# Key lengths in RWKV-7 on Trainium2: a product with block-diagonal ones in place of a product, a broadcast and a transpose

## The chip, the cores and the metric

One core of one Trainium2 chip runs the whole program. The core has five engines that run side by side, each through its own list in order: TensorE (PE, with its weight loads shown apart as PEld), VectorE (DVE), ScalarE (ACT), GpSimd (POOL) and SyncE (SP, which here only issues transfers). The metric is the time of one execution on the device in microseconds (us); lower is better.

## The reference, cut to what matters

Two layers of a decoder with three groups of heads; the change touches the RWKV-7 group alone (6 heads of 64 channels, 2048 tokens). Its part of the reference:

```python
kk = heads(k * k_k)
kk = kk / jnp.maximum(jnp.sqrt(jnp.sum(kk * kk, axis=-1, keepdims=True)), 1e-12)
k = k * (1.0 + (a - 1.0) * k_a)
r, k, v, a = heads(r), heads(k), heads(v), heads(a)
decay = jnp.exp(-jnp.exp(heads(w)))
y = _wkv7_scan(r, decay, k, v, -kk, kk * a)
```

`kk` is the removal key: each head's key, divided by its length. The scan uses it twice, as `-kk` and as `kk * a`; the kernel leaves one of the two undivided and puts the whole factor, one over the squared length, on the other.

## The kernel before, in words

Each layer has a first phase, `phase_a`, and then attention and the output projection. `phase_a` projects the input (each projection is 24 or 16 matmuls on line L441, into one of two PSUM banks), and beside that runs the RWKV group. Everything is written as chains, Python generators that yield the time at which they may go on, and `weave` picks the chain that is due next by a modelled clock (`clk`), in which each piece of work has a written cost. The order in which the chains are picked is the order of the instructions on PE, which is kept as written; the order on DVE, ACT and POOL is set by the scheduler of the tile framework. So a changed cost or a wait that is gone moves PE's whole order from that place on.

The RWKV group has these chains: `rwkv_prep` (a preparation: 128 tokens, so 4 for each block of 512 tokens, 16 for each layer, 32 in all), `rwkv_chunks` (two chunks of 64 tokens for each preparation), `rwkv_inv` (a triangular inverse, many small DVE rows, L689 and L691), `rwkv_run` (the state, one chunk after another) and `rwkv_out`. A block's fourth preparation comes late in the block's projections (`PACE`), near the next block's `norm`, in which PE transposes the normed input (L370) and DVE splits it (L269).

A preparation keeps channels on partitions and tokens along the row: a tile `[128, 3, 128]`, two heads on the 128 partitions, three such pairs. The sum over a head's 64 channels is therefore a sum over partitions, which PE makes. Before, `sq` (the squared key) is the stationary side and `ones2` (128 x 2) the moving side (L546), so that tokens come out on partitions, 6 numbers each. DVE bounds and inverts these (L548, L549), ACT spreads each over 64 columns (L551, `nb`), and PE transposes `nb` back (L592) into a PSUM bank `nps`. DVE multiplies that with `ke` into half of `bd` (L610); the other half is L611. Two more PE steps end a preparation: the product for the bonus (L620, of `rk`, which DVE makes on L617) and the transpose of `v` (L628). `bd` goes to the chunks' first product (L647). All small PSUM tiles of this chain take one of two banks (`MB`).

Of the kernel before, what the change touches and what calls it, by code (L numbers as in the profile page):

```python
# [10 lines left out]
F32 = mybir.dt.float32  # L11
# [3 lines left out]
AF = mybir.ActivationFunctionType  # L15
ALU = mybir.AluOpType
# [20 lines left out]
NP = RH // 2  # L37
# [14 lines left out]
RSB, XB, TRB = 6, 3, 7  # L52
# [7 lines left out]
MB, LMB, CHB, YB, PJ, HT = (0, 1), (2,), (3,), (4,), (5, 6), (7,)  # L60
# [130 lines left out]
def trunk(tc, a, out):  # L191
# [7 lines left out]
    def mk(p, shape, tag, dt=F32, bufs=None):  # L199
        return p.tile(list(shape), dt, name=tag, tag=tag, bufs=bufs)  # L200

    cst = pool(top, "cst")
# [6 lines left out]
    ident = cst.tile([128, 128], F32, name="ident")  # L209
    P.memset(ident, 0.0)  # L210
    P.affine_select(ident, ident, [[1, 128]], ALU.not_equal, 1.0, base=0, channel_multiplier=-1)
    ones2 = cst.tile([128, 2], F32, name="ones2")
    V.memset(ones2, 0.0)
    V.memset(ones2[0:64, 0:1], 1.0)
    V.memset(ones2[64:128, 1:2], 1.0)
    ones1 = cst.tile([128, 1], F32, name="ones1")
    V.memset(ones1, 1.0)
    mhalf = cst.tile([128, 1], F32, name="mhalf")
# [75 lines left out]
    def phase_a(l, rq_t, near, far, flags):  # L294
# [26 lines left out]
        for h in range(2):  # L321
            sl = HEADS[h]
# [186 lines left out]
        def rwkv_prep(j, u, q2, xin):  # L509
# [31 lines left out]
            t_ta = banks.give(b1, clk.a(128, e, times=3))  # L541
            yield from banks.wait(MB, 1, lambda: t_sq)

            sps, b = banks.get(MB, [128, 6])
            for p_ in range(NP):
                T.matmul(sps[:, 2 * p_:2 * p_ + 2], sq[:, p_], ones2, start=True, stop=True)  # L546
            n2 = mk(rt, [128, 6], "n2")
            V.tensor_scalar(n2, sps, 1e-24, None, ALU.max)  # L548
            V.reciprocal(n2, n2)  # L549
            nb = mk(rt, [128, 6, 64], "tr", bufs=TRB)  # L550
            A.activation(nb, n2.unsqueeze(2).to_broadcast([128, 6, 64]), AF.Copy, scale=-0.5)  # L551
            t = banks.give(b, clk.v(6, clk.pe(650)))
            t_nb = clk.a(384, clk.v(40, t))
            t = clk.v(384, clk.v(192, t_th))
            t_em = clk.a(460, t, times=2)
            V.tensor_scalar(th, th, 1.0, None, ALU.add)
# [29 lines left out]
                V.tensor_scalar(km[:, p_], ta[:, p_], ka[:, p_:p_ + 1], ka1[:, p_:p_ + 1], ALU.mult, ALU.add)  # L586
            V.tensor_tensor(km, km, k, ALU.mult)
            t_km = clk.v(384, clk.v(180, t_ta, times=3))
            yield from banks.wait(MB, 1, lambda: t_nb)
            nps, b = banks.get(MB, W3)  # L590
            for p_ in range(NP):
                T.transpose(nps[:, p_], nb[:, 2 * p_:2 * p_ + 2].rearrange("p a b -> p (a b)"), ident)  # L592
            e = clk.pe(330)
            t_ke = clk.v(384, max(t_ta, t_em), times=2)
            t_bd = banks.give(b, clk.v(384, max(t_ke, t_km, e), times=6))
            ke = mk(rt, W3, "tr", bufs=TRB)
            V.scalar_tensor_tensor(ke, ta, 1.0, kq, ALU.add, ALU.mult)
            V.tensor_tensor(ke, ke, em, ALU.mult)
# [2 lines left out]
            def c4(x):  # L601
                return x.rearrange("p a (c t) -> p c a t", c=2)
# [4 lines left out]

            bd = mk(rt, [128, 2, NP, 2, CH], "bd", bufs=2)
            for h, sl in enumerate(HEADS):
                V.tensor_tensor(bd[sl, :, :, h], c4(nps)[sl], c4(ke)[sl], ALU.mult)  # L610
                V.tensor_tensor(bd[sl, :, :, 1 - h], c4(km)[sl], c4(em)[sl], ALU.mult)  # L611
            yield lambda: done["out"] >= len(halves) - 2
            t_rk = clk.v(384, t_km)
# [121 lines left out]
        def rwkv_run(cur, s0, s1, y, odd):  # L735

            W = [128, NP, CH]
            xs1 = mk(rt, W, "x1")
            yield from banks.wait(CHB, 1, lambda: cur["t"])
            ps, b = banks.get(CHB, [128, 2, NP, CH])  # L740
            for p_ in range(NP):
                by_head(ps[:, 0, p_], cur["ar"][:, p_, 0], s0[:, p_], start=True, stop=True)
            V.tensor_tensor(xs1, ps[:, 0], cur["xv"], ALU.add)
            yield clk.v(192, clk.pe(520))
            for p_ in range(NP):
                by_head(ps[:, 1, p_], cur["T"][:, p_], xs1[:, p_], start=True, stop=True)
            uv = cur["uv"]
            for h, sl in enumerate(HEADS):
                V.tensor_copy(uv[sl, :, h], ps[sl, 1])
            t = banks.give(b, clk.v(192, clk.pe(520), times=2))  # L750
            yield from banks.wait(CHB, 1, lambda: t)
            ps, b = banks.get(CHB, [128, 2, NP, CH])
            for p_ in range(NP):
                for h, sl in enumerate(HEADS):
                    T.matmul(ps[sl, 0, p_], cur["bk"][:, p_, sl], uv[:, p_, h], start=True, stop=True)
            sp_ = mk(rt, W, "sp")
            V.tensor_tensor(sp_, ps[:, 0], s0, ALU.add)
            V.tensor_tensor(s1, sp_, cur["pc"].unsqueeze(2).to_broadcast(W), ALU.mult)
            t = clk.v(192, banks.give(b, clk.v(192, clk.pe(520))))
            yield from banks.wait(YB)  # L760
            py, b = banks.get(YB, [128, NP, CH])
            outs_ = [HEADS[(h + odd) % 2] for h in range(2)]
            for p_ in range(NP):
                for sl, so in zip(HEADS, outs_):
                    T.matmul(py[so, p_], cur["ar"][sl, p_, 1], s0[sl, p_], start=True, stop=False)
                for h, so in enumerate(outs_):
                    T.matmul(py[so, p_], cur["mr"][:, p_, h], uv[:, p_, h], start=False, stop=True)
            for h, so in enumerate(outs_):
                A.copy(y[so, :, h], py[so])
            ty = banks.give(b, clk.a(192, clk.pe(700), times=2))  # L770
            yield t
            return ty
# [841 lines left out]
```

## Time and profile before

| what | value |
|---|---|
| median of 3 runs | 4171.56 us (4166.28 to 4175.11) |
| the profiled execution's own time | 4180.67 us |
| its span (first to last instruction) | 4178.9 us |
| PE busy | 3693.0 us (88%) |
| DVE busy | 2775.8 us (66%) |
| ACT busy | 1917.1 us (46%) |
| POOL busy | 1439.5 us (34%) |
| mean granted TensorE clock | 0.945 |

The profile is of one execution. Its span is shorter than its time by what lies before the first and after the last instruction, 1.8 us. Busy shares are averages over stages; in this kernel `phase_a` of the first layer runs from about 0 to 1050 us, that of the second from about 2090 to 3110 us, and every line that the change touches lies in these two.

### The profile page before, as it was taken

What the parts mean: (1) busy time and instruction counts of PE and PEld (TensorE: products, weight loads), DVE (VectorE), ACT (ScalarE), POOL (GpSimd) and SP (SyncE); (2) the same over time, 40 slices, a digit from 0 to 9 for tenths busy, and PEclk for the clock granted to TensorE, in tenths of its full rate; (3) what the DMA queues carried; (4) which work ended last, traced back from release to release, by engine and by line L of the source; (5) the groups of instructions that cost most, each with busy time, mean ns of one, the idle gap of its engine ahead of it and who ended that gap; (6) DMA issues with size and microseconds to landing.
All of it is one profiled execution on the core that took longest, in us unless ns stands there. A gap on an engine that the chain in (4) does not pass through costs nothing. (4 is left out here: it accounts for less than half of the span.)

```text
span 4178.9 us, 76529 instructions
## 1 busy us (share of the span) xinstructions
PE 3693.0 (88%) x27232; PEld 2965.5 (71%) x27232; DVE 2775.8 (66%) x7444; ACT 1917.1 (46%) x4506; POOL 1439.5 (34%) x1684
## 2 busy tenths in 40 slices
PE   6999999899878888989899899998988789888699
PEld 5767777676656777777777677676766677777577
DVE  3775667756758888973346776666666688888643
ACT  3444444443456666651143444444434566666511
POOL 3434344443223334421143443443422243344211
PEclk9999999999989999999999999999989899999899
DMA  4533444334465654636444444343343555445254
GB/s 113 134 98 97 108 107 119 85 105 119 125 175 171 166 157 141 180 102 199 141 109 114 106 109 109 86 127 83 106 108 111 147 158 170 129 141 157 88 180 137
DMA packets 681630, 534.69 MB, mean 128 GB/s; under 512 B 233344, under 2 KB 585120, under 8 KB 681248
## 3 DMA queue, kind: packets, MB, share of 16 engines
q1 hardware_dynamic: 636704, 506.20, 43.6%
q10 hardware_dynamic: 40448, 11.02, 1.3%
q0 software_dynamic: 4096, 12.59, 0.9%
q8 instruction: 215, 3.52, 0.4%
q14 instruction: 167, 1.37, 0.1%
HBM read 417.43 MB, written 112.21 MB: 127 GB/s over the span
## 5 line engine op out<-in xcount | busy, mean ns | idle before, releaser
L441 PE MATMUL b<-h,wh 128*128 128x512 f32 x3584 | 1212.5, 413 | 49.4 <-DVE xk L470 16.1
L397 POOL TENSOR_TENSOR wl<-raw,wh 128x512 fp32r<-128x512 f32 x440 | 601.9, 1371 | 739.1 <-ACT wh L396 639.6
L441 PEld LDWEIGHTS b<-h,wh 128*128 128x128 f32 x3584 | 682.9, 194 | 218.0 <-DVE xk L470 18.7
L441 PE MATMUL b<-h,wl 128*128 128x512 f32 x1760 | 723.7, 411 | 2.1 <-POOL wl L397 1.9
L1137 ACT ACTIVATE row<-row,mx 128x1024 f32<-128x1024 f32 (+6 forms) x480 | 428.9, 895 | 231.4 <-DVE mx L1129 229.6
L396 ACT CAST wh<-raw 128x512 fp32r<-128x512 f32 x448 | 273.4, 614 | 517.2 <-PE b L441 328.0
L1062 PE MATMUL b<-ident,row 128*128 128x128 f32 x2720 | 390.7, 292 | 132.3 <-DVE row L1427 55.0
L1062 PEld LDWEIGHTS b<-ident,row 128*128 128x128 f32 x2720 | 330.8, 150 | 176.8 <-DVE row L1427 35.1
L441 PEld LDWEIGHTS b<-h,wl 128*128 128x128 f32 x1760 | 340.7, 194 | 79.3 <-POOL wl L397 5.1
L1126 PE MATMUL b<-k,q 128*128 128x512 f32 (+3 forms) x1440 | 372.3, 388 | 22.9 <-DVE mx L1129 14.7
L1126 PEld LDWEIGHTS b<-k,q 128*128 128x128 f32 x1440 | 254.0, 198 | 74.8 <-DVE mx L1129 22.0
L689 DVE TENSOR_TENSOR am<-w 48x30 f32<-48x30 f32 (+14 forms) x480 | 229.4, 478 | 90.9 <-DMA w<-linv 78.3
L1064 ACT COPY row<-b 128x512 f32<-128x512 f32 (+3 forms) x433 | 203.7, 505 | 112.0 <-PE b L1062 101.6
L1064 DVE COPY row<-b 128x512 f32<-128x512 f32 (+3 forms) x367 | 220.3, 623 | 49.7 <-PE b L1062 46.7
L1429 POOL TENSOR_SCALAR tmp<-tmp,cf 128x512 f32<-128x512 f32 (+2 forms) x144 | 117.4, 820 | 368.2 <-DVE cf L1418 246.5
L1072 PE MATMUL b<-row,v 128*64 128x128 f32 x3264 | 226.0, 286 | 12.9 <-ACT row L1064 7.5
L691 DVE TENSOR_TENSOR w<-w,am 48x30 f32<-48x30 f32 (+14 forms) x480 | 222.4, 463 | 12.7
L1072 PEld LDWEIGHTS b<-row,v 128*64 128x64 f32 x3264 | 200.6, 143 | 36.0 <-ACT row L1064 11.3
L1126 PE MATMUL b<-dk,dq 128*128 128x512 f32 (+3 forms) x640 | 199.2, 399 | 22.2 <-DVE mx L1129 11.9
L1562 PE MATMUL b<-wo,m 128*128 128x512 f32 x512 | 206.2, 403 | 0.0
L1137 ACT ACTIVATE tmp<-tmp,mx 128x1024 f32<-128x1024 f32 (+2 forms) x192 | 171.3, 894 | 72.9 <-DVE mx L1129 72.6
L1564 PE MATMUL b<-wo,m 128*128 128x512 f32 x512 | 203.6, 398 | 0.0
(279 smaller groups left out, 6727.5 us busy)
## 6 DMA issues: line engine op xcount, KB each, us to landing
raw<-in_w_in_dram SPq DMA_DIRECT2D x432, 256.0 KB
lq<-lat SPq DMA_DIRECT2D x192, 256.0 KB
d<-dist SPq DMA_DIRECT2D x70, 512.0 KB
lk<-lat SPq DMA_DIRECT2D x48, 512.0 KB
x<-in_x_dram SPq DMA_DIRECT2D x32, 512.0 KB
gat<-st SPq DMA_DIRECT2D x64, 256.0 KB
dk<-dqk SPq DMA_DIRECT2D x128, 128.0 KB
dq<-dqk SPq DMA_DIRECT2D x256, 64.0 KB
```

The source lines that it names most:

```text
L396: A.copy(hi[:, :, 0:m], raw[:, :, 0:m])
L397: P.tensor_tensor(lo[:, :, 0:m], raw[:, :, 0:m], hi[:, :, 0:m].bitcast(F32), ALU.subtract)
L441: T.matmul(ps[0:w], x[k // 4][:, k % 4, 0:w], y, start=(k == 0 and i == 0), stop=(k == KD - 1 and i == len(ops) - 1))
L689: V.tensor_tensor(t, w[:, 0:s, s:s + 1].to_broadcast([48, n, m]), w[:, s:s + 1, s + 1:SB].to_broadcast([48, n, m]), ALU.mult)
L691: V.tensor_tensor(w[:, 0:s, s + 1:SB], w[:, 0:s, s + 1:SB], t, ALU.add)
L1062: T.transpose(tp[:, k * 128:(k + 1) * 128], row.at(512 * c_ + 128 * k, 128), ident)
L1064: (V.tensor_copy if eng == "V" else A.copy)(row.at(512 * c_, 128 * n), tp[:, 0:128 * n])
L1072: T.matmul(o[HEADS[qi]], vget(kb), row.at(kb * 128, 128), start=(kb == 0), stop=(kb == 2 * g + qi))
L1126: T.matmul(ps[:, 0:n], x, y, start=(i_ == 0), stop=(i_ == len(ops) - 1))
L1137: A.activation(row.at(1024 * h, n), row.at(1024 * h, n), AF.Exp, bias=mx0, scale=-1.0, accum_out=lsum[:, h:h + 1])
L1562: T.matmul(ps, m[0][:, k], wo[0][:, k, hs], start=(k == 0), stop=False)
L1564: T.matmul(ps, m[1][:, k], wo[0][:, k, hs], start=False, stop=(k == KD - 1))
```

## The change

The two sides of the product are swapped and `ones2` becomes 128 x 128 with two blocks of ones on its diagonal. Each channel then gets its head's sum in its own place, already spread over the head's 64 channels, and nothing has to be turned back. DVE bounds, scales and inverts 384 elements for each partition (L548, L549) where it did 6; the broadcast on ACT (L551) and the three transposes (L592) with their wait for a bank are gone; `bd` is made from `nb` in SBUF. The modelled costs are rewritten to match (two DVE steps of 384). The tile `sp` of `rwkv_run` is given the tag `x1`, so that it shares the space of `xs1`, which makes room for the larger `ones2`.

```diff
-    ones2 = cst.tile([128, 2], F32, name="ones2")
+    ones2 = cst.tile([128, 128], F32, name="ones2")
     V.memset(ones2, 0.0)
-    V.memset(ones2[0:64, 0:1], 1.0)
-    V.memset(ones2[64:128, 1:2], 1.0)
+    V.memset(ones2[0:64, 0:64], 1.0)
+    V.memset(ones2[64:128, 64:128], 1.0)
...
-            sps, b = banks.get(MB, [128, 6])
+            sps, b = banks.get(MB, W3)
             for p_ in range(NP):
-                T.matmul(sps[:, 2 * p_:2 * p_ + 2], sq[:, p_], ones2, start=True, stop=True)
-            n2 = mk(rt, [128, 6], "n2")
-            V.tensor_scalar(n2, sps, 1e-24, None, ALU.max)
-            V.reciprocal(n2, n2)
-            nb = mk(rt, [128, 6, 64], "tr", bufs=TRB)
-            A.activation(nb, n2.unsqueeze(2).to_broadcast([128, 6, 64]), AF.Copy, scale=-0.5)
-            t = banks.give(b, clk.v(6, clk.pe(650)))
-            t_nb = clk.a(384, clk.v(40, t))
+                T.matmul(sps[:, p_], ones2, sq[:, p_], start=True, stop=True)
+            nb = mk(rt, W3, "tr", bufs=TRB)
+            V.tensor_scalar(nb, sps, -2.0, -2e-24, ALU.mult, ALU.min)
+            V.reciprocal(nb, nb)
+            t_nb = clk.v(384, banks.give(b, clk.v(384, clk.pe(650))))
...
-            yield from banks.wait(MB, 1, lambda: t_nb)
-            nps, b = banks.get(MB, W3)
-            for p_ in range(NP):
-                T.transpose(nps[:, p_], nb[:, 2 * p_:2 * p_ + 2].rearrange("p a b -> p (a b)"), ident)
-            e = clk.pe(330)
             t_ke = clk.v(384, max(t_ta, t_em), times=2)
-            t_bd = banks.give(b, clk.v(384, max(t_ke, t_km, e), times=6))
+            t_bd = clk.v(384, max(t_ke, t_km, t_nb), times=6)
...
-                V.tensor_tensor(bd[sl, :, :, h], c4(nps)[sl], c4(ke)[sl], ALU.mult)
+                V.tensor_tensor(bd[sl, :, :, h], c4(nb)[sl], c4(ke)[sl], ALU.mult)
...
-            sp_ = mk(rt, W, "sp")
+            sp_ = mk(rt, W, "x1")
```

Lines behind the edit have lower numbers after the change: L610 (`bd` from the lengths) becomes L602, L611 L603, L617 (`rk`) L609, L620 (its product) L612, L647 L639, L757 and L758 (the new state) L749 and L750.

The order moves with it. The first place is PE's list around the fourth preparation of the first layer's second block. `b_...` is a PSUM bank's tile, `h`, `wh` and `wl` are the operands of a projection, `x` is the input that `norm` transposes, and `tr` is any of the preparation's tiles. Before the change:

```order
L546 MATMUL b_5000<-ones_65,tr 128x2 x3
...
L592 MATMUL b_5097<-ident,tr 128x128 x3
L441 MATMUL b_5070<-h,wh 128x512
...
L507 MATMUL b_5135<-state_284,ar 64x64 x6
L441 MATMUL b_5070<-h,wl 128x512
L370 MATMUL b_5152<-ident,x 128x128 x4
L370 MATMUL b_5159<-ident,x 128x128 x4
L793 MATMUL b_5166<-ident,yy 128x128 x3
L507 MATMUL b_5135<-x_5134,g_286 64x64 x6
L370 MATMUL b_5190<-ident,x 128x128 x4
L370 MATMUL b_5197<-ident,x 128x128 x4
L620 MATMUL b_5206<-tr,rkb 128x128 x3
```

The same place after the change:

```order
L546 MATMUL b_5004<-tr,ones_65 128x128 x3
L441 MATMUL b_4867<-h,wl 128x512
L370 MATMUL b_5070<-ident,x 128x128 x4
L370 MATMUL b_5077<-ident,x 128x128 x4
L747 MATMUL b_5084<-uv,bk 64x64 x6
...
L785 MATMUL b_5109<-ident,yy 128x128 x3
L370 MATMUL b_5125<-ident,x 128x128 x4
L370 MATMUL b_5132<-ident,x 128x128 x4
L507 MATMUL b_5140<-state_284,ar 64x64 x6
L612 MATMUL b_5150<-tr,rkb 128x128 x3
```

Between the two products of the preparation (L546, and L620 or L612) stood 26 matmuls of projections; now there is one, and the block's projections all stand ahead of L546. Counted in the same way, the fourth preparations of the first layer's four blocks had 50, 26, 37 and 49 matmuls of L441 there and now have 47, 1, 1 and 6; those of the second layer had 47, 1, 23 and 1 and now have 37, 0, 0 and 0. The other 24 preparations had 31 to 60 and have 28 to 65.

The second place is DVE's list in the same preparation, from the length's first row to the product `rk`. After the change:

```order
L548 TENSOR_SCALAR tr<-b_5004 128x384
...
L749 TENSOR_TENSOR x_5091<-b_5084,state_283 128x192
L549 RECIPROCAL tr<-tr 128x384
L269 TENSOR_TENSOR h<-b_5077,h 128x4x128
L583 TENSOR_SCALAR tr<-tr,ka,ka_266 128x128 x3
...
L750 TENSOR_TENSOR state_284<-x_5091,pc 128x192
...
L269 TENSOR_TENSOR h<-b_5125,h 128x4x128
L269 TENSOR_TENSOR h<-b_5132,h 128x4x128
...
L609 TENSOR_TENSOR tr<-xr,tr 128x384
```

Before the change the same stretch reads:

```order
L548 TENSOR_SCALAR n_5004<-b_5000 128x6
L757 TENSOR_TENSOR sp<-b_5072,state_283 128x192
L549 RECIPROCAL n_5004<-n_5004 128x6
L1023 SCALAR_TENSOR_TENSOR st<-st,b_4872 128x512
L758 TENSOR_TENSOR state_284<-sp,pc 128x192
L558 SCALAR_TENSOR_TENSOR tr<-rstm,tr 128x384
...
L617 TENSOR_TENSOR tr<-xr,tr 128x384
```

The reciprocal over 384 elements now stands between the two rows that make the next state (L749 and L750), and four splits of the next block's input (L269), one ahead of the reciprocal and three behind it, have come in ahead of `rk`. In all 32 preparations the reciprocal stands ahead of every other step that follows the scan (L555).

## Rows read from the trace of the kernel before

**Rows 1.** Windows of the two first phases: busy us (instructions) by engine, clock, DMA, GB/s.
```profile
110.00:1050.00 940.00, 866.49 (x6378) 669.63 (x6376) 620.98 (x1509) 399.68 (x915) 372.76 (x378) 0.96 0.42 108
2090.00:3110.00 1020.00, 948.24 (x6671) 729.01 (x6670) 663.58 (x1549) 433.52 (x990) 409.66 (x422) 0.95 0.41 106
```

**Rows 2.** Line L551: who waited for it (us, times).
```profile
  PE b L592: 19.1, 11
```

**Rows 3.** PE in order of time, then a window's busy times and clock.
```profile
445.86 0.90 PE L592 MATMUL b<-ident,tr 128*128 128x128 f32 x3 [4.31 <-ACT tr L551]
...
445.80:449.20 3.40, 3.34 (x11) 2.77 (x12) 3.40 (x10) 1.13 (x3) 0.00 (x0) 0.57 0.00 0
```

**Rows 4.** Lines L592, L546, L620: count, then ns min/median/max; L620's wait (us, times).
```profile
L592 PEld LDWEIGHTS b<-ident,tr x96: 137/141/231, 114.0 to 3101.5; 128*128 128x128 f32 x96
...
L546 PE MATMUL b<-ones,tr x192: 165/251/273, 112.2 to 3098.0; 128*128 128x2 f32 x192
...
L620 PE MATMUL b<-tr,rkb x192: 270/275/582, 122.5 to 3109.4; 128*128 128x128 f32 x192
...
  DVE tr L617: 4.9, 5
```

**Rows 5.** DVE groups by shape: count, busy us, mean ns of one, idle before.
```profile
L611 DVE TENSOR_TENSOR bd<-tr 64x384 f32<-64x384 f32 x64 | 49.7, 776 | 0.4
...
L610 DVE TENSOR_TENSOR bd<-b,tr 64x384 f32<-64x384 f32 x64 | 35.3, 552 | 0.6
...
L622 DVE TENSOR_TENSOR bv<-b,xv 128x384 f32<-128x384 f32 x32 | 17.7, 553 | 14.1 <-PE b L620 13.6
...
L556 DVE TENSOR_SCALAR tr<-tr 128x384 f32<-128x384 f32 x32 | 12.1, 377 | 10.3 <-ACT tr L528 10.0
...
L548 DVE TENSOR_SCALAR n<-b 128x6 f32<-128x6 f32 x32 | 5.4, 168 | 18.1 <-PE b L546 17.6
```

**Rows 6.** The three sizes of reciprocal: count, then ns min/median/max, first and last start.
```profile
L1417 DVE RECIPROCAL cf<-dls x128: 136/159/170, 1198.3 to 3935.1; 128x1 f32<-128x1 f32 x128
...
L1318 DVE RECIPROCAL li<-ls x96: 140/161/170, 1056.7 to 3933.5; 128x2 f32<-128x2 f32 x96
...
L549 DVE RECIPROCAL n<-n x32: 165/191/194, 113.1 to 3100.4; 128x6 f32<-128x6 f32 x32
```

**Rows 7.** PE in order of time, fourth preparation of the second block (start, us long).
```profile
508.64 0.83 PE L546 MATMUL b<-ones,tr 128*128 128x2 f32 x6
...
513.07 0.55 PE L592 MATMUL b<-ident,tr 128*128 128x128 f32 x3 [0.72 <-ACT tr L551]
...
518.67 0.56 PE L507 MATMUL b<-state,ar 64*64 64x64 f32 x12
...
519.50 1.03 PE L370 MATMUL b<-ident,x 128*128 128x128 f32 x8
520.37 0.49 PE L793 MATMUL b<-ident,yy 128*128 128x128 f32 x3
...
524.27 1.49 PE L620 MATMUL b<-tr,rkb 128*128 128x128 f32 x6
```

**Rows 8.** DVE in order of time, the same preparation.
```profile
511.94 0.17 DVE L548 TENSOR_SCALAR n<-b 128x6 f32<-128x6 f32 x1
...
519.38 1.07 DVE L617 TENSOR_TENSOR tr<-xr,tr 128x384 f32<-128x384 f32 x1
...
522.38 0.69 DVE L269 TENSOR_TENSOR h<-b,h 128x512 fp32r<-128x512 f32 x1
```

**Rows 9.** The first and the last of the 32 preparations, DVE and PE.
```profile
120.87 1.53 DVE L617 TENSOR_TENSOR tr<-xr,tr 128x384 f32<-128x384 f32 x1
...
122.45 0.94 PE L620 MATMUL b<-tr,rkb 128*128 128x128 f32 x6
...
3107.59 0.55 DVE L617 TENSOR_TENSOR tr<-xr,tr 128x384 f32<-128x384 f32 x1
...
3108.20 1.65 PE L620 MATMUL b<-tr,rkb 128*128 128x128 f32 x6 [1.15 <-DVE tr L617]
```

## The prediction

> **What bounds the kernel now.** I read the page first, then the busy times by stage, then who waits for whom on the changed lines, then the instructions in order of time around single preparations. All that is changed lies in the two first phases. There PE is busy for 866.5 of 940 us and 948.2 of 1020 us, DVE for 621 and 664, at a granted clock of 0.96 and 0.95 [rows 1]. PE is the bound, but it works through its list in order: it loses time where the next instruction waits for a result, 74 and 72 us in these two windows. So two questions decide: how much PE work goes, and where PE will stand and wait. The reader is to see that one such wait is removed: PE waits at the transposes L592 for ACT's broadcast, 11 times and 19.1 us in all [rows 2], the longest 4.31 us [rows 3]. Behind that wait the clock is 0.57 for 3.4 us, most of it the lower level [rows 3], which costs another (1 - 0.57) x 3.4 = 1.5 us.
>
> **PE's work.** Gone are 96 transposes. Their matmuls are pipelined behind the weight loads, so I price them by these: 96 x 0.141 = 13.5 us [rows 4]. The sums' product has the same 192 records after the change, with 128 columns each instead of 2. Its twin is L620, which has just that shape: 275 ns against 251, at most 192 x 0.024 = 4.6 us [rows 4]. Both stand behind equal weight loads, so between 0 and 4.6 I take 2. Gone too are the 19.1 us of waiting [rows 2], and with them clock: at 1.5 us for 4.3 us of waiting this is 6.7 us; 0 if short waits don't lower the clock. Together -13.5 + 2 - 19.1 - 6.7 = -37 us. ACT's broadcasts go as well; since ACT isn't waited for elsewhere on this path, I count nothing for them.
>
> **DVE's work.** The bounding step reads 384 elements from PSUM where it read 6. L622 is the nearest row, 0.553 us against 0.168 for L548 [rows 5]: +0.39 us. `bd` from the lengths now has both sources in SBUF, as L611 has: 0.776 against 0.552 us [rows 5], so +0.45 us for the two of a preparation. The reciprocal over 384 elements has no row. From below it costs what a one-source step over 384 elements in SBUF does, 0.377 us [rows 5]. From above I take the sizes that the trace has: medians of 159, 161 and 191 ns for 1, 2 and 6 elements [rows 6]. From 2 to 6 that is 30 ns for 4 elements, 7.5 ns each, and on that line 384 elements take 0.191 + 378 x 0.0075 = 3.0 us. From 1 to 6 it is 6.4 ns each and 2.6 us. Between L548 and L622 an ordinary step takes (553 - 168) / 378 = 1.0 ns for an element [rows 5], so the six-element row speaks for the slow end, though 30 ns is a small lever for so long a line. I take 3.0, since the nearest sizes give it, and keep 0.38 to 3.0 for the range. A preparation's product `rk` then comes 0.39 + (3.0 - 0.19) = 3.2 us later on DVE, `bd` 3.65 us later. In all 32 this is 117 us of DVE work at 3.0 and 33 us at 0.38.
>
> The Trainium skill ("VectorE: DVE Perf Modes", section "First, the fixed hardware budget") speaks against this change: it says that the reciprocal is an iterative divide with a repeat count of 8. With eight cycles for an element at the 0.96 GHz that the same page gives, 384 elements would take 3.2 us, an estimate from that page, and the sum below would rise by some 2 us over 3.0 and by some 36 us over 0.38. Six elements would then take 42 ns more than one; the medians show 32, so the trace comes near it without settling it.
>
> **Where the 3 us go.** DVE works in order, so the reciprocal holds up all that stands behind it: the state of `rwkv_run` (L750), the splits of the input and `rk`. Cover is what PE has to do meanwhile. In the trace of before it is mostly there. In the second block's fourth preparation `rk` ends at 520.45 and PE comes to it at 524.27 [rows 7, 8], 3.8 us of slack; in the first of the 32 preparations the slack is 0.05 us, in the last PE waits 1.15 us [rows 9]; over all 32 PE waited 4.9 us at L620 [rows 4].
>
> *Fourth preparations.* In four of eight blocks the change takes the cover away: of 26, 37, 49 and 23 projection matmuls between the two products 1, 1, 6 and 0 are left. For the second block PE's list between them is now: what stood from 508.64 to 513.07 (4.4 us, less a wait of 0.7 and two projection matmuls, some 0.5, so 3.2), 16 transposes (2 x 1.03), 0.49 and 0.56 [rows 7]: 6.3 us. DVE took 8.5 us there from L548 to the end of L617 [rows 8]; added are 3.2 us and four splits of 0.69 [rows 8], so 14.5 us, and it starts 0.83 us after PE's product did [rows 7]. PE comes 14.5 + 0.83 - 6.3 = 9.0 us too early. Four such blocks make 36 us. Two more had 1 matmul there and now have none; they waited already and only get the 3.2 us: 6 us. Together 42 us, or 27 us with the cheap reciprocal (4 x 6.4 and 2 x 0.6).
>
> *The other 26.* They keep 28 to 65 projection matmuls. Set against the slack between the end of L617 and L620, of which rows 9 show the first and the last of 32 preparations, 3.2 us would exceed it in about six, by some 15 us in all; I take 20 us, since PE also comes earlier now. The bounds are 0 and 60: below, if PE's other waits cover it, and above, 26 x (3.2 - 0.9), if most of the delay reaches PE through the state's rows.
>
> *Clock.* Six waits of 4 us or more at 1.5 us each: +9 us [rows 3].
>
> **The sum.** -37 + 42 + 20 + 9 = +34 us on the profiled execution's 4180.7, which is 4214.7. That execution is 9.1 us above the median of the runs shown, 4171.6; against the median I forecast 4206 us, 0.8% slower.
>
> `sp` sharing the space of `xs1` I cost at nothing: the state's row needs PE's product, which has read `xs1` long before, and the next `xs1` needs that state anyway. If this were wrong, each of the 64 chunks would add a DVE step's wait of some 0.3 us to the chain of states.
>
> **Rivals.** *The reciprocal is cheap* (0.38 us). For it speaks that one and two elements differ by 2 ns [rows 6]; against it the six-element row. Then -37 + 27 + 3 + 5 = -2: 4170 us, no change. Chance 0.17.
>
> *The uncovered places cost little, and the kernel is faster.* The projections that stood under the fourth preparations aren't lost, they are done earlier; and at a block's edge PE waits for the splits of `norm` anyway. If of the 42 us only 18 are new waiting and the other preparations hide theirs, -37 + 18 + 4 = -15: 4156 us. It decides once a block's edge costs under about 5 us each (six of them, with 4 us of clock, against 37). Against it speaks that DVE's list there is 14.5 us of work with the splits in the middle of it. Chance 0.18.
>
> *DVE binds more widely.* With 117 us more, DVE's share of the two phases goes from 66% to 72%, and `rwkv_run` meets the reciprocal between its rows in many places. With 60 us for the other 26 and clock in step (+27), -37 + 42 + 60 + 27 = +92: 4264 us. For it speaks that PE's projections need POOL's splits of the weights, and DVE and POOL already slow each other: L611 with two SBUF sources takes 776 ns on the mean, L610 with one 552 [rows 5]. Chance 0.15.
>
> The Trainium skill ("SBUF — State Buffer", section "Who interferes with whom") has the rule for it: a DVE instruction with two SBUF inputs and a GpSimd instruction that reads SBUF exclude each other for their whole length. By it the 64 rows of L602 join those of L611; without it they would stay at 0.55 us and the sum would lose 14 us of DVE work, of which I count 2 on PE. The mean of L611 agrees with it.
>
> **How the numbers follow.** My forecast has 0.5. The range reaches from below the rival that ends faster to the one in which DVE binds: 4148 to 4262 us, leaving out half of the latter and the ends of both. The forecast's own range is 4180 to 4235, from 0 to 45 us for the other 26 preparations. This kernel can tell a difference of 0.2%, 8 us, from none. Slower by more: 0.92 of the forecast, all of the wide DVE bound, a quarter of the cheap reciprocal: 0.65. Within: 0.05 of the forecast, 0.45 of the cheap one, a fifth of the faster rival: 0.14. Faster: the rest, 0.21.
>
> **What would show it.** The reciprocal of L549 near 3 us (below 1 us the cheap rival stands); L602 near 0.78 us; no row on L551 or L592; PE waiting several us each at L612, at the transposes L370 or at the state's product L507 in the fourth preparations, with low clock behind; little waiting at L612 in the others. The prediction is wrong if PE's waits in the first phases sum to less than before, or if the projections now ahead of the fourth preparations shorten the phase by as much as the edges lengthen it.

## The result, and the profile after

The changed kernel takes 4211.56 us (median of 4 runs, 4207.31 to 4216.21) against 4173.34 us for the kernel before in the same session: the ratio is 1.0085, with a 95% interval of 1.0071 to 1.0099. That is slower by 0.85%, where 0.8% and 4206 us were forecast. The profiled execution took 4210.32 us.

First the changed rows: groups of instructions by shape of the changed kernel, VectorE (DVE) and TensorE (PE); the columns are those of [rows 5].

```profile
L549 DVE RECIPROCAL tr<-tr 128x384 f32<-128x384 f32 x32 | 81.1, 2534 | 0.0
L603 DVE TENSOR_TENSOR bd<-tr 64x384 f32<-64x384 f32 x64 | 48.2, 753 | 0.4
L602 DVE TENSOR_TENSOR bd<-tr 64x384 f32<-64x384 f32 x64 | 41.6, 650 | 0.7
L548 DVE TENSOR_SCALAR tr<-b 128x384 f32<-128x384 f32 x32 | 17.8, 555 | 16.7 <-PE b L546 16.5
...
L546 PE MATMUL b<-tr,ones 128*128 128x128 f32 x192 | 28.9, 289 | 4.2 <-ACT tr L528 4.2
```

The reciprocal over 384 elements, the price that had no row before, is 2.53 us. The bounding step is 0.56 us, as its neighbour L622 was [rows 5].

Next, what TensorE waited for in the changed kernel (line, what it waited for: us in all, times, longest us).

```profile
PE b L612 <- DVE tr L609: 60.9, 20, 6.1
...
PE b L507 <- DVE state L750: 14.8, 6, 3.9
```

The 19.1 us of waiting at the transposes [rows 2] are gone with them. In their place TensorE now stands 60.9 us at the product `rk` (L612, which was L620), where it stood 4.9 us before with the weight loads' waits counted in [rows 4]. L609 is the multiplication on DVE that makes this product's operand, and it stands behind the reciprocal in DVE's list.

The third view is the busy time by stage, in four stretches whose borders are the last projection matmul of a layer's first phase and the first preparation of the second layer. A row has the stretch, its length, then the busy time of PE, PEld, DVE, ACT and POOL, the clock, the DMA share and GB/s. First the kernel before, with its own borders:

```profile
110.00:1029.30 919.30, 852.19 (x6240) 658.56 (x6238) 609.37 (x1460) 391.13 (x889) 366.72 (x371) 0.96 0.41 106
1029.30:2164.50 1135.20, 985.42 (x7333) 819.08 (x7332) 752.08 (x2207) 554.03 (x1327) 344.72 (x467) 0.93 0.52 153
2164.50:3099.10 934.60, 867.14 (x6289) 665.31 (x6287) 636.39 (x1497) 398.17 (x920) 376.21 (x376) 0.96 0.41 105
3099.10:4178.90 1079.80, 913.85 (x7064) 763.52 (x7063) 745.07 (x2187) 533.56 (x1299) 309.36 (x398) 0.93 0.49 142
```

And the changed kernel:

```profile
110.00:1037.60 927.60, 847.93 (x6182) 654.38 (x6180) 644.67 (x1445) 379.56 (x869) 365.05 (x373) 0.95 0.40 106
1037.60:2174.20 1136.60, 986.96 (x7347) 818.49 (x7346) 759.82 (x2218) 558.90 (x1338) 345.69 (x467) 0.93 0.52 153
2174.20:3135.50 961.30, 871.91 (x6220) 669.04 (x6218) 665.69 (x1489) 390.12 (x902) 370.84 (x375) 0.94 0.39 102
3135.50:4208.50 1073.00, 907.25 (x7086) 758.21 (x7084) 748.64 (x2191) 535.34 (x1306) 313.10 (x399) 0.93 0.49 143
```

The reader is to see where the time went: the two first phases are 8.3 and 26.7 us longer, the other two stretches 1.4 us longer and 6.8 us shorter. PE's idle time (length less busy time) grows from 67.1 to 79.7 us and from 67.5 to 89.4 us, 34.5 us together. Its busy time stays where it was (1719.3 and 1719.8 us for the two phases together), although 96 transposes are gone: the sums' product L546 takes 28.9 us where it took 24.4, and the granted clock is lower, 0.95 and 0.94 for 0.96 in both. These are single executions: the two other stretches, which the change hardly touches, came out between 1128 and 1145 us and between 1063 and 1085 us in the 14 kernels of this document.

The place that the prediction worked out, the fourth preparation of the second block, is here in order of time, first PE and then DVE of the changed kernel (start, us long; in brackets how long the engine was idle before and for whom).

```profile
525.13 0.55 PE L785 MATMUL b<-ident,yy 128*128 128x128 f32 x3 [1.25 <-ACT yy L761]
...
530.40 0.91 PE L507 MATMUL b<-state,ar 64*64 64x64 f32 x12 [3.85 <-DVE state L750]
535.85 1.65 PE L612 MATMUL b<-tr,rkb 128*128 128x128 f32 x6 [4.54 <-DVE tr L609]
```
```profile
521.97 0.56 DVE L548 TENSOR_SCALAR tr<-b 128x384 f32<-128x384 f32 x1
...
524.75 2.54 DVE L549 RECIPROCAL tr<-tr 128x384 f32<-128x384 f32 x1
...
530.00 0.35 DVE L750 TENSOR_TENSOR state<-x,pc 128x192 f32<-128x192 f32 x1
...
535.23 0.56 DVE L609 TENSOR_TENSOR tr<-xr,tr 128x384 f32<-128x384 f32 x1
```

PE waits 1.25 + 3.85 + 4.54 = 9.64 us in this stretch, the first of the three for ScalarE. Before, it came to this product without a wait [rows 7], after 2.4 us of waiting at other places since the sums' product.

### The profile page after: what moved, and what is told of

Same layout as the page of the kernel before. It is cut to its first block, busy times and chain, and to the rows that moved or that the text cites. A ratio compares the mean times of both kernels' runs of the same rounds, so it can differ in the third digit from the quotient of the medians.

```text
span 4208.5 us, 76290 instructions
## 1 busy us (share of the span) xinstructions
PE 3688.8 (88%) x27136; PEld 2959.3 (70%) x27136; DVE 2850.9 (68%) x7435; ACT 1903.9 (45%) x4483; POOL 1435.9 (34%) x1684
## 5 line engine op out<-in xcount | busy, mean ns | idle before, releaser
L441 PE MATMUL b<-h,wh 128*128 128x512 f32 x3584 | 1206.6, 413 | 40.9 <-DVE xk L470 14.0
L397 POOL TENSOR_TENSOR wl<-raw,wh 128x512 fp32r<-128x512 f32 x440 | 590.7, 1345 | 760.5 <-ACT wh L396 671.3
L441 PEld LDWEIGHTS b<-h,wh 128*128 128x128 f32 x3584 | 679.5, 193 | 207.9 <-DVE xk L470 17.4
L441 PE MATMUL b<-h,wl 128*128 128x512 f32 x1760 | 722.2, 410 | 1.3 <-POOL wl L397 1.1
L441 PEld LDWEIGHTS b<-h,wl 128*128 128x128 f32 x1760 | 340.0, 193 | 81.2 <-POOL wl L397 5.3
L683 DVE TENSOR_TENSOR w<-w,am 48x30 f32<-48x30 f32 (+14 forms) x480 | 224.4, 468 | 12.6
```

The costliest lines, as they stand in the source:

```text
L397: P.tensor_tensor(lo[:, :, 0:m], raw[:, :, 0:m], hi[:, :, 0:m].bitcast(F32), ALU.subtract)
L441: T.matmul(ps[0:w], x[k // 4][:, k % 4, 0:w], y, start=(k == 0 and i == 0), stop=(k == KD - 1 and i == len(ops) - 1))
L683: V.tensor_tensor(w[:, 0:s, s + 1:SB], w[:, 0:s, s + 1:SB], t, ALU.add)
```

## The experiments

The kernel before was run beside each on the same chip, at a median of 4182 us; the ratios below are to it. Single profiled executions of one kernel lie up to some 14 us from its median, so sizes are taken from the ratios, and the profile's rows tell the places. Stretches of two profiles are compared only to see in which layer a difference lies.

**The reciprocal alone taken away.** In the changed kernel a one-source operation that writes a constant stands in the reciprocal's place; the removal keys' lengths are left out. PE's order is that of the changed kernel.

```diff
-            V.reciprocal(nb, nb)
+            V.tensor_scalar(nb, nb, 0.0, -1e-6, ALU.mult, ALU.add)
```

> The changed kernel with the reciprocal of 384 elements replaced by an ordinary one-source step of the same size that writes a constant, so the key's length is left out of the result; PE's order stays that of the changed kernel. Theory (the loss is half the 2.5 us reciprocal, half the order that took the projections away from under the fourth preparations): the step takes about 0.4 us, PE's wait at the bonus product falls from 61 us to about 25 us, and the time comes to about 4175 us, near the kernel before. Rival A (the reciprocal is all of it): 4140 us, the removed transposes and waits show in full. Rival B (the order is all of it): 4205 us.

It took 4187.64 us, ratio 1.0011 (1.0001 to 1.0021). The wait at the product `rk`:

```profile
PE b L612 <- DVE tr L609: 26.1, 10, 6.8
```

This is near the theory, in the time and in the wait. So of the 0.85%, 0.74% (31 us) go with the reciprocal. What is left of the change gains nothing.

**The reciprocal added.** In the kernel before, a reciprocal over 384 elements behind the scan, whose result nobody reads. To make room for its result, `sp` shares the space of `xs1` here as in the change.

```diff
+            dum = mk(rt, W3, "dum", BF16)
...
+                V.reciprocal(dum, cum)
...
-            sp_ = mk(rt, W, "sp")
+            sp_ = mk(rt, W, "x1")
```

> The kernel before with one more reciprocal over 384 elements behind the scan in each preparation, whose result nobody reads; PE's order is that of before. Theory: the 2.5 us are only partly covered, PE's waits at the bonus product and the state's product grow by some 25 us, time about 4198 us. Rival A (under the old order the cover is there, it is the order that costs): within 5 us of the kernel before, 4173 us. Rival B (the reciprocal costs PE all its length): 32 x 2.5 = 80 us, 4253 us.

It took 4232.3 us, ratio 1.0119 (1.0103 to 1.0134): 50 us, about twice the theory's 25 and under rival B's 80. What PE waited for (here L595 is the transposes, L623 the product `rk`, L631 the transposes of `xv` and L671 the product on `la`):

```profile
PE b L595 <- ACT tr L551: 20.7, 11, 4.4
PE b L631 <- DVE bd L613: 14.5, 10, 3.8
PE b L623 <- DVE tr L620: 12.9, 7, 3.8
PE b L671 <- DVE mr L654: 10.5, 5, 3.8
```

The old order had no cover for 2.5 us of DVE either: the wait on ACT stays, and three products that waited little now wait for DVE.

**The changed kernel in the old order.** The modelled times and the bank use of before, so that PE's list is that of before without the transposes; the reciprocal stays.

```diff
-            t_nb = clk.v(384, banks.give(b, clk.v(384, clk.pe(650))))
+            t = banks.give(b, clk.v(6, clk.pe(650)))
+            t_nb = clk.a(384, clk.v(40, t))
...
+            yield from banks.wait(MB, 1, lambda: t_nb)
+            b = min(MB, key=lambda b: banks.free[b])
+            banks.free[b] = math.inf
+            e = clk.pe(330)
...
-            t_bd = clk.v(384, max(t_ke, t_km, t_nb), times=6)
+            t_bd = banks.give(b, clk.v(384, max(t_ke, t_km, e), times=6))
```

> The changed kernel with the modelled times of before (and a pretended use of the bank for the transposes), so that PE's list is that of before without the transposes; DVE's work is that of the change, the reciprocal included. Theory: the fourth preparations of three of four blocks get their projections back, PE's wait at the bonus product is about 35 us in place of 61, time about 4178 us. Rival A (order does not matter, the reciprocal does): 4211 us, as changed. Rival B (the order is all of the loss): 4140 us.

It took 4217.6 us, ratio 1.0079 (1.0067 to 1.0091), the same as the changed kernel. The wait at the product `rk` (L617 here):

```profile
PE b L617 <- DVE tr L614: 38.8, 14, 5.8
```

With the reciprocal in the kernel, giving the old cover back gains nothing. In the eight fourth preparations PE's idle time between the two products is 34.1 us, where the changed kernel has 52.5; but over the two phases it is 172.2 us for 169.1, so the waiting stands elsewhere. The theory that the order was a large part fell with this run.

**Old order and cheap step**, the fourth corner: the two edits together.

> The changed kernel in the order of the kernel before, with a one-source operation of 0.25 us in place of the 2.54 us reciprocal; the step writes a constant, so the removal keys' lengths are left out. It is the fourth corner beside the changed kernel, the cheap step in the new order and the reciprocal in the old order. Theory (the reciprocal costs about 30 us in either order and the order nearly nothing): ratio 1.0005, between 0.997 and 1.003, 0.7% below the old order with the reciprocal. Rival (the old order's cover is worth the 42 us that the prediction put on the fourth preparations, once no reciprocal stands in the way): ratio 0.992, between 0.989 and 0.996.

It took 4163.41 us, ratio 0.9958 (0.9945 to 0.9971). Its wait at the product `rk`, then its two first phases:

```profile
PE b L617 <- DVE tr L614: 25.0, 8, 6.4
```
```profile
110.00:1029.20 919.20, 843.84 (x6199) 648.92 (x6199) 628.19 (x1461) 383.93 (x875) 375.81 (x373) 0.97 0.41 107
...
2160.60:3091.20 930.60, 854.99 (x6244) 656.24 (x6242) 648.36 (x1498) 389.61 (x905) 384.84 (x376) 0.97 0.41 105
```

The four corners:

| ratio to before | old order | new order |
|---|---|---|
| cheap step | 0.9958 | 1.0011 |
| reciprocal | 1.0079 | 1.0085 |

The expectation was wrong in two ways: the reciprocal costs 1.21% (51 us) in the old order and 0.74% (31 us) in the new one, and the new order costs 0.53% (22 us) with the cheap step and 0.06%, less than the noise, with the reciprocal. The ratio lies in the rival's range. The costs of order and reciprocal don't add. And with neither of them the rest of the change, with its longer bounding step and the cheap step (0.39 us) still on DVE, is worth 0.42%, 18 us: TensorE is 8.35 and 12.15 us less busy in the two phases, but more idle (75.4 and 75.6 us against 67.1 and 67.5). About as much waiting as went at the transposes (19.1 us) has come at the product `rk`: 25.0 us, where it was 4.9. Only 4.1 us of the 18 lie in the two phases of the profiles; the other stretches, which the change hardly touches, are 13.5 us shorter. So what the removed parts give back is known no better than as 4 to 18 us.

The same two phases of the cheap step in the new order:

```profile
110.00:1013.70 903.70, 840.24 (x6185) 646.20 (x6184) 615.31 (x1446) 379.75 (x870) 368.35 (x373) 0.97 0.41 109
...
2149.80:3112.40 962.60, 876.19 (x6220) 672.36 (x6218) 636.91 (x1489) 389.52 (x901) 368.89 (x375) 0.94 0.39 102
```

The new order is 15.5 us better than the old in the first layer and 32.0 us worse in the second; the stretch behind each is 4.7 us longer, so a part may only have moved behind the border with the layer's last preparation. Of these 32.0 us, 10.8 are idle time of PE and 21.2 are busy time, at a clock of 0.94 against 0.97. With the phases of the changed kernel in both orders (its own above, the old at the end of this document) the layers can be told apart. In the first, the reciprocal costs 26.8 us in the old order and 23.9 in the new. In the second it costs 21.2 us in the old order and nothing in the new (961.3 us against 962.6). So it is in the second layer that the two costs don't add.

**Which part of the modelled costs makes the new order dear.** The cheap step, with the old modelled time of the lengths, but without the pretended bank and transposes. The lengths are left out here too.

```diff
-            t_nb = clk.v(384, banks.give(b, clk.v(384, clk.pe(650))))
+            t = banks.give(b, clk.v(6, clk.pe(650)))
+            t_nb = clk.a(384, clk.v(40, t))
```

> The cheap step (which writes a constant, so the lengths are left out) with the modelled time of the kernel before for the lengths (a ScalarE step behind two six-element ones), but without the pretended wait for a bank, the 0.33 us of TensorE and the bank held until the removal keys are made: half of what differs between the cheap step in the new order (ratio 1.0011) and in the old (0.9958). Theory A (the order loses its cover through the removed bank and TensorE time): ratio 1.001, between 0.9995 and 1.0035. Rival B (through the earlier time of the lengths): ratio 0.996, between 0.994 and 0.9985. The layer to look at is the second, where the two corners differ by 32 us (962.6 against 930.6 us in the second layer's preparations).

It took 4164.68 us, ratio 0.9956 (0.9942 to 0.9969): rival B. The order loses through the earlier time that the model gives to the lengths, not through the bank and the 0.33 us of TensorE that are gone. With the old time the fourth preparations have 26, 37 and 35 projection matmuls again between the two products in the first layer's last three blocks, and 6, 6 and 25 in the second's. The wait at the product `rk` (L613) and the second layer's first phase:

```profile
PE b L613 <- DVE tr L610: 40.5, 16, 7.9
```
```profile
2160.90:3092.30 931.40, 858.27 (x6279) 657.62 (x6278) 652.58 (x1517) 394.67 (x913) 382.78 (x376) 0.97 0.41 105
```

This wait is longer than the 26.1 us of the cheap step in the new order, and the kernel is 0.55% faster. So one line of the waits doesn't price an order; the phase's length does.

**A true price in the model.** The writer of the order is told 2535 ns for the reciprocal.

```diff
-            t_nb = clk.v(384, banks.give(b, clk.v(384, clk.pe(650))))
+            t_nb = clk.run(banks.give(b, clk.v(384, clk.pe(650))), "V", 2535)
```

> The changed kernel, but the writer of the order charges 2.54 us of VectorE for the step and the reciprocal over 384 elements (the 2535 ns of the reciprocal's row after the change) in place of one 384-element operation. No instruction is added or removed. Theory (VectorE's 2.5 us ahead of the removal keys costs the time, and the order can give only a part of it back): ratio to the kernel before 1.006, between 1.004 and 1.0085, and the wait of the rk product on VectorE's L609 falls from 60.9 us to about 40. Rival (the loss comes from an order made with a wrong price): ratio 1.001, as with the cheap step, and that wait under 25 us.

It took 4234.44 us, ratio 1.0128 (1.0114 to 1.0141), slower than either expected, though the wait fell as the theory had it:

```profile
PE b L612 <- DVE tr L609: 41.0, 16, 8.7
PE b L639 <- DVE bv L614: 20.4, 7, 4.2
```

**And a later place for the product `rk`.** The same, with one line more.

```diff
-            t_rk = clk.v(384, t_km)
+            t_rk = clk.v(384, max(t_km, t_bd))
```

> As the kernel with the true price, and the order also gives the rk product a time behind the removal-key products, where VectorE's own queue has it, so that TensorE takes other products first. Theory (the 2.5 us are lost wherever TensorE meets VectorE next): the wait at the rk product falls under 25 us but waits at the next products on VectorE (those on bd, mr and the state) grow by about as much; ratio 1.006, between 1.004 and 1.0085. Rival (one place in the order costs it): ratio 1.000 to 1.002, and no other wait grows by over 10 us.

It took 4245.13 us, ratio 1.015 (1.0136 to 1.0165). Both expectations missed it: the wait at the product fell to 33.5 us only, and the kernel got slower. Moving PE's work with the model is no way to hide the reciprocal here; why these two orders are as bad as they are wasn't found. Neither gives the fourth preparations their cover back: of the six that have next to none in the changed kernel, only one, in the second run, has more than 6 projection matmuls between the two products.

**The reciprocal behind the operand of `rk` on VectorE.** In the old-order kernel the multiplication of `r` and `km` is written ahead, and DVE issues the reciprocal behind it.

```diff
-            V.reciprocal(nb, nb)
...
             V.tensor_tensor(km, km, k, ALU.mult)
+            rk = mk(rt, W3, "tr", bufs=TRB)
+            i_ = V.tensor_tensor(rk, r, km, ALU.mult)
+            with tc.issue_after(i_.ins):
+                V.reciprocal(nb, nb)
...
-            rk = mk(rt, W3, "tr", bufs=TRB)
-            V.tensor_tensor(rk, r, km, ALU.mult)
```

> The whole change with the reciprocal, TensorE in the order of the kernel before, and VectorE told to issue the reciprocal behind the multiplication of r by the keys that feeds the rk product (in the old-order run it stands ahead of the scan). Same operations. Theory A (the reciprocal costs time because the rk product's operand stands behind it in VectorE's queue): the wait at the rk product falls from 38.8 us to about the 25.0 us of the old order with the cheap step, later products (on bd and la) wait a few us more; ratio to the kernel before 1.002, between 0.999 and 1.005. Rival (VectorE's 2.5 us delay whatever comes next, bd's products in place of the rk product): ratio 1.007, between 1.005 and 1.009, the wait only changes its line.

It took 4195.31 us, ratio 1.003 (1.0018 to 1.0042): theory A. (In the old-order run the reciprocal stood behind the scan, not ahead of it, and ahead of `rk`, in all 32 preparations; here it stands behind `rk` in all.) The product `rk` (L618) and the first product on `bd` (L645):

```profile
PE b L645 <- DVE bd L610: 20.8, 16, 3.2
...
PE b L618 <- DVE tr L586: 17.6, 7, 4.6
```

The reciprocal takes as long as before on DVE, but 20 us (1.0079 to 1.003) are gone with the new order of DVE's list. The two waits together are no shorter than the 38.8 us at the product `rk` before; it is PE's idle time over the two phases that fell, from 172.2 to 153.3 us. The edit does two things, it moves the reciprocal back and the multiplication for `rk` forward, and no run tells them apart. Some 30 us remain (0.9958 to 1.003).

**The same edit in the changed kernel's order.**

> The changed kernel, its own order of TensorE, with the same edit: the reciprocal behind the multiplication that feeds the rk product. Theory A: the wait at the rk product falls from 60.9 us to about the 26.1 us of the cheap step; ratio 1.003, between 1.001 and 1.006. Rival: ratio 1.0085, between 1.007 and 1.010, waits of equal size at the products on bd.

It took 4203.16 us, ratio 1.0052 (1.0034 to 1.007), inside theory A's range. The waits were:

```profile
PE b L640 <- DVE bd L605: 13.4, 10, 4.6
PE b L613 <- DVE tr L585: 12.8, 4, 6.4
```

The wait fell by more than expected, from 60.9 to 12.8 us, the time by 14 us only.

**Another way to drop ScalarE's broadcast.** In the kernel before, PE spreads the six reciprocals itself, with a stride of zero in the stationary operand.

```diff
-            V.tensor_scalar(n2, sps, 1e-24, None, ALU.max)
+            V.tensor_scalar(n2, sps, -2.0, -2e-24, ALU.mult, ALU.min)
...
-            nb = mk(rt, [128, 6, 64], "tr", bufs=TRB)
-            A.activation(nb, n2.unsqueeze(2).to_broadcast([128, 6, 64]), AF.Copy, scale=-0.5)
...
-            t_nb = clk.a(384, clk.v(40, t))
+            t_nb = clk.v(6, t)
...
-                T.transpose(nps[:, p_], nb[:, 2 * p_:2 * p_ + 2].rearrange("p a b -> p (a b)"), ident)
+                for h, sl in enumerate(HEADS):
+                    T.matmul(nps[sl, p_], n2[:, 2 * p_ + h:2 * p_ + h + 1].to_broadcast([128, 64]), ident, start=True, stop=True)
```

> The kernel before without the broadcast on ACT: six numbers are still inverted, and the product that turns them back reads each as a stationary side with a stride of zero (six products with 64 columns in place of three transposes). Theory: no long reciprocal and a shorter way from the sums to the product; PE's waits there fall from 19 us to under 10, PE gains some 14 us of work, DVE is as before: 4160 us. Rival A: PE's waits there only move to the next place and the added PE work counts, 4185 us. Rival B: the moved order takes cover away elsewhere, 4200 us.

It took 4254.86 us, ratio 1.017 (1.0153 to 1.0187), slower than any of the three expectations; PE stood 58.8 us at the product:

```profile
PE b L591 <- DVE n L549: 58.8, 17, 7.2
```

With the old modelled times (`t_nb` as in the kernel before):

> The kernel before without ScalarE's broadcast; TensorE spreads the six reciprocals itself by a product with a stride of zero, as in the spread run, but the order is made with the modelled times of the kernel before, that is with a time for ScalarE's step that no longer exists. Same instructions as the spread run. TensorE is busier by 17.5 us (37.6 against 20.1 us at the spreading products). Theory (the spread run lost its time because the order brought TensorE to the product too early): the 58.8 us of waiting on the step's VectorE work fall under 15 us, ratio 1.001, between 0.998 and 1.004. Rival (TensorE waits for VectorE there in any order): wait over 40 us, ratio 1.012 or more.

It took 4211.61 us, ratio 1.007 (1.0058 to 1.0081), and the wait was 45.5 us, so the modelled time was only a part. DVE's rows of the first preparation of that kernel show the rest:

```profile
113.97 0.96 DVE L556 TENSOR_TENSOR_SCAN tr<-rstm,tr 128x384 f32<-128x384 bf16 x1
114.85 1.93 DVE L584 TENSOR_SCALAR tr<-tr,ka,ka 128x128 f32<-128x128 f32 x1
116.70 0.15 DVE L548 TENSOR_SCALAR n<-b 128x6 f32<-128x6 f32 x1
...
117.75 0.18 DVE L549 RECIPROCAL n<-n 128x6 f32<-128x6 f32 x1
```

With the step on ACT gone, the two small steps stand behind the scan and the keys' first operations (L548 in the middle of L584, L549 two rows later). Told to issue them first:

```diff
-            V.reciprocal(n2, n2)
+            i_ = V.reciprocal(n2, n2)
...
-            V.tensor_scalar(th, th, 1.0, None, ALU.add)
+            with tc.issue_after(i_.ins):
+                V.tensor_scalar(th, th, 1.0, None, ALU.add)
```

> The spread run with the old modelled times, and VectorE told to issue the two six-element steps ahead of the addition to the decays, as it does in the kernel before; in the spread runs they stand behind the scan and the keys' first operations. Theory A (the spread lost its time in VectorE's queue): the wait at the spreading products falls from 45.5 us to under 15, TensorE stays 17.5 us busier than with the transposes, ScalarE's 19.1 us wait is gone: ratio 1.000, between 0.997 and 1.003. Rival (the products' own cost): ratio 1.005, between 1.003 and 1.008.

It took 4189.67 us, ratio 1.0018 (1.0006 to 1.0029), with 12.6 us of waiting for those steps at that product (and 9.0 us more for ScalarE, where the kernel before had 2.9). Theory A, and the same lesson as with the reciprocal: DVE's own order was worth 0.5% twice. Of the versions run, none that keeps the whole computation beats the kernel before.

## Why the prediction was right, step by step

- **The total was right, 0.85% for 0.8%, and so was the main cause**, DVE's reciprocal in front of what PE waits for. The prediction's own sums can be set beside the corners. With the cheap step in the new order it had -2 us, measured +5 (0.11%). With the reciprocal on top it had 36 us more, measured 31. That the total came within 2 us of the forecast is luck in part, as the terms below show.
- **PE's work: one term failed.** The -37 us were to be what the removed parts give back. The corner without the reciprocal and without the new order gave 18, of which the profiles show 4 in the two phases. The step that failed is "Gone too are the 19.1 us of waiting": in that corner PE waits 25.0 us at the product `rk`, the next in its list whose operand DVE makes, and it is 16.4 us more idle over the two phases than before. PE's busy time in the two phases is 20.5 us lower, for 18.2 in the sum (13.5 less 2, and 6.7), but not for the reason given: the clock rose from 0.96 to 0.97 though the waits had not become shorter. In the changed kernel the sums' product costs 28.9 us, 4.5 more than before, the top of its bounds.
- **The reciprocal: 2.54 us, for 3.0 taken.** The line from one to six elements, which the prediction named as 2.6, was the better one. The Trainium skill ("VectorE: DVE Perf Modes", section "First, the fixed hardware budget") names a repeat count of 8; the prediction's estimate from it was 3.2 us, and the measured 2.535 us lie 0.7 below. It pointed the right way, and the rival of a cheap reciprocal is out.
- **`bd` from the lengths: 0.650 us on the mean, for 0.776 taken**; its median is 0.554, so most rows don't slow down with both sources in SBUF. The Trainium skill ("SBUF — State Buffer", section "Who interferes with whom") has it that such a row and a GpSimd row that reads SBUF contend. The trace agrees: all of the 7 rows over 0.62 us have a GpSimd row beside them (the rows are in the last section).
- **DVE's work:** the changed rows have 93.8 us more (75.1, 12.4 and 6.3 for the reciprocal, the bounding step and `bd`), for 117. DVE's whole busy time grew by 75.1 us, since other rows became shorter.
- **The fourth preparations: the size right, the reason incomplete.** In the place worked out PE waits 9.64 us for 9.0 forecast, of which 2.4 were there before. Over the six fourth preparations of the 42 us, PE's idle time between the two products grew by 37 us, from 12.5 to 49.5. But the old order, with its cover, costs the same with the reciprocal in it (1.0079), so the 42 us were not the price of lost cover: what is gained there is lost elsewhere. With the cheap step the new order costs 22 us, for 27 forecast with a cheap reciprocal, but it does so in the second layer only, while in the first layer, where three of the six lie, the new order gains. The faster rival's argument, that projections done earlier aren't lost, holds there.
- **The other 26 preparations: 20 us taken, 27 more of idle time between the two products.** The 15 us under that figure held two fourth preparations (0.05 and 0.06 us of slack before) that the 42 us already count; without them the slack gives 9. Of the 60.9 us of waiting at L612, the eight fourth preparations have 20.5 us (4.54, 3.57 and 0.69 in the first layer, 1.21, 1.92, 2.48 and 6.13 in the second, one without) and the other 24 the rest. A wait at one line isn't its price, as the runs above show.
- **The clock: +9 less 6.7 taken.** Over the two phases PE's busy time is 0.5 us higher, where its instructions alone would make it some 9 us lower (-13.5 and +4.5): about 9 us, for 2 in the sum. The lower clock would explain them; no run shows it alone.

So two errors met. By the corners, what the change gives back was put 19 us too high, and what order and reciprocal cost together (71 us forecast, 53 measured from 0.9958 to 1.0085) 18 us too high. The two phases of the profiles tell the same: PE's idle time was to grow by 43 us (-19, 42 and 20) and grew by 34.5, its busy time was to fall by 9 us and rose by 0.5. (The forecast's own range, 4180 to 4235, is 4186 to 4231 by its own terms.)

Open stays why the second layer is slower in the new order at a clock of 0.94, and why the two orders with other modelled prices are so much slower. The shared space of `sp`, which the sum has at nothing, was not tried alone; the run with the reciprocal added has it too.

## What to carry to other kernels

A wait removed from an engine that works in order is gained only if the next product's operand is ready; here as much waiting came at a later product as had gone. A small step that is widened has to be priced at its own rate for each element and at its place in the queue: half a per cent lay in which of two operations DVE issued first. When a change alters both a cost and an order, all four corners are to be run, since the two costs need not add.

## What the runs showed of the hardware

From 191 ns for 6 elements [rows 6] to 2535 ns for 384 the reciprocal takes 6.2 ns for an element, about six times the 1.0 ns of an ordinary step [rows 5]; the medians for 1 and 2 elements lie within 5 ns of that line, and no run has a size between 6 and 384. With a bf16 destination it is the same, 2.55 us. The two lines, the changed kernel's by count and ns (min/median/max), then the one added to the kernel before:

```profile
L549 DVE RECIPROCAL tr<-tr x32: 2520/2535/2552, 116.8 to 3141.2; 128x384 f32<-128x384 f32 x32
```
```profile
L562 DVE RECIPROCAL dum<-tr 128x384 bf16<-128x384 f32 x32 | 81.5, 2548 | 0.7
```

The rows that make `bd` with both sources in SBUF took longer only beside a GpSimd row. Of the 64 rows L602 of the changed kernel 7 took more than 0.62 us, and GpSimd had a row running during every one; of the other 57, 15 had one beside them too. Before, with one source in PSUM, none of the 64 rows L610 took over 0.57 us, though 22 had a GpSimd row beside them. By count and ns (min/median/max), before and after:

```profile
L610 DVE TENSOR_TENSOR bd<-b,tr x64: 535/555/562, 122.8 to 3110.0; 64x384 f32<-64x384 f32 x64
```
```profile
L602 DVE TENSOR_TENSOR bd<-tr x64: 539/554/1792, 127.0 to 3152.1; 64x384 f32<-64x384 f32 x64
```

One of the seven in order of time (start, us long): of two rows L602 the second takes 1.56 us and ends 0.42 us after a GpSimd row (POOL) that splits a weight.

```profile
221.92 2.12 DVE L602 TENSOR_TENSOR bd<-tr 64x384 f32<-64x384 f32 x2
```
```profile
222.04 1.58 POOL L397 TENSOR_TENSOR wl<-raw,wh 128x512 fp32r<-128x512 f32 x1 [0.65 <-ACT wh L396]
```

PE's busy time and its waits stand in no fixed proportion. From the cheap step to the reciprocal in the old order, with the same number of PE instructions, PE's idle time in the two phases grew by 21.2 us and its busy time by 26.8 us, at a granted clock of 0.95 for 0.97. From the kernel before to the changed one, 34.5 us more of idle time went with about 9 us of clock; and from the kernel before to the cheap step in the old order, PE was 16.4 us more idle at a higher clock, 0.97 for 0.96. The two first phases of the changed kernel in the old order, beside those of the cheap step above:

```profile
110.00:1056.00 946.00, 854.98 (x6200) 659.05 (x6199) 652.25 (x1461) 384.09 (x875) 366.92 (x373) 0.95 0.40 104
...
2187.10:3138.90 951.80, 870.65 (x6244) 667.12 (x6242) 670.69 (x1498) 390.07 (x906) 368.40 (x376) 0.95 0.39 103
```
